# A three-fold fetch of sample operands, issued as three transfers of 32 rows

## The chip, the cores and the metric

The kernel runs on one core of a Trainium2 chip. The metric is the device time of one launch in microseconds (us), the median of several runs. The engines work side by side, each through its own list of instructions in order: TensorE (PE in the profile, its weight loads PEld), VectorE (DVE), ScalarE (ACT), GpSimd (POOL) and SyncE (SP), which here does nothing but issue transfers.

## The reference

One inference step of a two-layer recurrent decoder trunk, on 256 prompt tokens (one sequence) and 64 sample tokens (8 sequences of 8 tokens), width 2048, all in float32. Layer 0 mixes with gated DeltaNet heads (8 of 128 x 128) and GLA heads (4 of 128 x 256); layer 1 is a gated linear recurrence (RG-LRU) with a short convolution. Each layer is a normalisation, one large input projection, the mixer, a gate, and an output projection added to x. The new recurrent states are outputs too. What matters here is the last step of the two mixers for a chunk of sample tokens, the new state:

```python
def _gated_delta_rule(q, k, v, g, beta, S0):
    ...
        S = S * jnp.exp(g_last)[..., None, None] + jnp.einsum('bhck,bhcv->bhkv', k_dec, v_new)

def _gla(q, k, v, gk, S0):
    ...
        S = S * jnp.exp(b_last)[..., None] + jnp.einsum('bhck,bhcv->bhkv', k_dec, v_c)
```

For the sample tokens that is, for each of 8 sequences and each head, the old state scaled by a decay, plus an outer product over 8 tokens.

## The kernel before

All 320 tokens stand as columns, features in partitions. The dense work is 30 groups of 512 output features; a group runs over 8 chunks of 256 input features (`run_group`). A chunk's weights (`wst`, 512 KB) come by one transfer of SyncE (line 209), are split into a rounded part `wh` on ScalarE (line 239) and a remainder `wl` on VectorE (line 240), and are multiplied on TensorE (line 264) with tokens split likewise into `xh` (line 1410) and `xl` (line 1411): three products per tile, `xh wh`, `xl wh` and `xh wl`, which give float32 accuracy. `wst` has three buffers, `wh` and `wl` six each.

Everything else is written as Python generators that hang in queues (`hi`, `lo`, `tails`). Between the matmuls of a group, `slot` advances the queues by one step each, and `wait("name")` lets a number of slots pass that a table gives. So the order of instructions on each engine comes from the order in which the program is traced, with priorities for a few pieces. `behind(i)` ties an instruction to the last matmul traced: it isn't put ahead of that matmul in the order, but it doesn't wait for it by a semaphore. All transfers of SyncE leave from one queue.

The generator `sample_states` computes the new states of the sample tokens. It runs twice in the queue `lo`: `sample_states(0, 16)` for the delta heads, beside the first output projection, and `sample_states(16, 24)` for GLA, beside the last one. Its operands were written earlier to small tensors in device memory, `kt_scratch` (k), `wv_scratch` (v) and `vk_scratch` (v and k together), by SyncE (`to_rows`, line 985): 32 rows of tokens, each of which holds four tokens' vectors one behind the other.

- `fetch` (line 996) loads one such piece into a tile of 96 partitions: the same 32 rows three times, at partitions 0, 32 and 64, by one transfer whose source pattern begins with three repeats of step zero. There are twelve of them: four `uk` and four `uv` (each 96 rows of 2 KB, 192 KB) and four `uvk` (96 rows of 3 KB, 288 KB). Each name has two buffers.
- `parts` casts the tile to the rounded form (`ukh`, `uvh`, `uvkh`; VectorE, line 1003), and GpSimd replaces one 32-row third by the remainder of k and another by that of v (line 1007), so that one product over 96 rows is the sum of the three products of a split multiplication.
- `spread` (line 1012, GpSimd) makes `uvm`, the v of one block of rows, masked so that one matmul gives four sequences.
- The matmul (line 1112 for delta, `sn`; line 1126 for GLA, `gsn`) gives the outer products, and VectorE adds the decayed old state (`ust`, `ugt`; lines 1116 and 1130). The states come in by SyncE (lines 1060 and 1066) and go out by GpSimd's queue (lines 1119 and 1133).

Of the kernel before, what the change touches and what calls it, by code (L numbers as in the profile page):

```python
# [71 lines left out]
def hybrid_step(ctx, tc, x_cols, w_dense, w_small, w_lr, w_gate, par_a, par_b, par_c, gains, head_rows,  # L72
# [3 lines left out]
    pe, act, dve, pool, sp = nc.tensor, nc.scalar, nc.vector, nc.gpsimd, nc.sync  # L76
# [49 lines left out]
    def behind(i):  # L126
        tc.add_manual_dep(i.ins, marks[-1].name, mybir.DependencyInfo(
            mybir.DependencyClass.NoSync, mybir.DependencyReason.DATA), reason="issue_after")
# [858 lines left out]
    def sample_states(first, last):  # L987
# [5 lines left out]
        def fetch(name, src, off, n, w, bufs):  # L993

            t = ws.tile([R, n, w], F32, name=name, tag=name, bufs=bufs)
            behind(sp.dma_start(t.rearrange("p q w -> p (q w)"), bass.AP(  # L996
                tensor=src.tensor, offset=src.offset + off, ap=[[0, 3], [4 * w, 32], [1, n * w]])))
            return t

        def parts(t, name, n, w, k, v):  # L1000
# [17 lines left out]
        def fetch_unit(v):  # L1018
            if v < 4:
                raw[v] = [fetch("uk", kt_d[v], 0, 4, P, 2), None]  # L1020
                yield from wait("sample_states.1")
                raw[v][1] = fetch("uv", wv_d[v], 0, 4, P, 2)
                yield from wait("sample_states.1")

        def fetch_half(i):
            if 2 * i < last:
                v, r = divmod(2 * i, 4)
                raw["g", i] = fetch("uvk", vk_d[v - 4], 3 * P * r, 2, 3 * P, 2)
# [886 lines left out]
    rows = fw.tile([P, NT], F32, name="frows")  # L1915
# [3 lines left out]
    for m, f, n in ((0, 0, 1), (0, 1, 1), (0, 2, 2), (1, 0, 2), (1, 2, 2), (2, 0, 2), (2, 2, 2), (3, 2, 2)):  # L1919
        t = ob[m][:, f:f + n]  # L1920
# [64 lines left out]
```

## Time and profile before

| | |
|---|---|
| runs | 998.79, 994.37, 994.74 us; median 994.74 |
| the profiled execution | 994.33 us, its span 992.6 us |
| TensorE busy | 969.5 us (98% of the span) |
| VectorE, ScalarE, GpSimd busy | 707.5, 532.9, 220.2 us |
| bytes moved | 171.62 MB, a mean of 173 GB/s |
| queue of SyncE (q1) | 59716 packets, 160.35 MB |

The profile shows one execution. Times within it count from the start of the span, and what the run takes beyond the span (1.73 us here) lies around it. A line such as "L996" is line 996 of the kernel. The text after the change reads single rows: an engine's timeline gives start, length, engine, line and operation with output and inputs, then in brackets how long the engine stood idle before it and which instruction or transfer is held to have released it.

### The profile page before, as it was taken

To read this page: it belongs to the slowest core of one execution; us is meant where nothing else is said; L and a number is where in the kernel's file an instruction comes from. 1 tells how busy PE (TensorE), PEld (TensorE's weight loads), DVE (VectorE), ACT (ScalarE), POOL (GpSimd) and SP (SyncE) were. 2 spreads that over 40 slices of the span, in tenths; PEclk is the share of its full clock that TensorE was granted. 3 is DMA by queue.
4 is the path that set the end of the run, shared out by engine and by line. 5 is a ranking of instruction groups with operands and counts; after the bars stand their busy time and mean duration, and the time that the engine had idled before them with its cause. 6 is when DMAs were issued, how large, how long until landed. Compare 5 with 4: busy or idle time off the path is not lost.

```text
span 992.6 us, 18768 instructions
## 1 busy us (share of the span) xinstructions
PE 969.5 (98%) x6917; PEld 950.5 (96%) x6917; DVE 707.5 (71%) x1485; ACT 532.9 (54%) x1083; POOL 220.2 (22%) x365
## 2 busy tenths in 40 slices
PE   9999999999999999999998999999999999999995
PEld 9989999999999999999978999999999999999995
DVE  7898887666545556779667789877969668766753
ACT  8556874457333444776423345447685885333441
POOL 4520018503282111120104234200010000052200
PEclk9999999999999999999999999999999999999998
DMA  8544444534455366445486877654545445568742
GB/s 297 178 134 135 133 130 157 143 131 135 127 157 163 93 218 228 133 111 151 157 258 204 241 258 229 228 165 146 158 124 189 130 127 169 165 216 276 258 155 106
DMA packets 64792, 171.62 MB, mean 173 GB/s; under 512 B 16345, under 2 KB 21997, under 8 KB 64189
## 3 DMA queue, kind: packets, MB, share of 16 engines
q1 hardware_dynamic: 59716, 160.35, 51.8%
q0 software_dynamic: 2720, 8.66, 2.3%
q10 hardware_dynamic: 2264, 1.42, 0.5%
q8 instruction: 54, 0.88, 0.4%
q14 instruction: 38, 0.30, 0.1%
HBM read 155.73 MB, written 14.68 MB: 172 GB/s over the span
## 4 chain that ended last, share of the span: by engine, by line
PE 44%; DVE 2%; DMA 2%; POOL 1%; issue 1%; SPq 0%; DVEq 0%; ACT 0%; POOLq 0%
PE acc L264 42%; DMA uv<-wv_scratch 1%; DMA ugt<-in_state_gla_dram 1%; POOL uvkh L1007 1%; DVE wl L240 1%; DVE ob L1921 0%; PE lg L1549 0%; PE lg L1550 0%; PE lg L1548 0%; PE gsn L1126 0%; PE sn L1112 0%; DVE xh L1410 0%; PE fsp L1670 0%; POOL gso L1166 0%; SPq L996 0%
## 5 line engine op out<-in xcount | busy, mean ns | idle before, releaser
L264 PE MATMUL acc<-xh,wh 128*128 128x320 f32 x1920 | 601.2, 313 | 2.7 <-DVE slab L355 1.2
L264 PE MATMUL acc<-xl,wh 128*128 128x320 f32 x1920 | 595.1, 310 | 1.3 <-DVE xl L1411 1.3
L264 PE MATMUL acc<-xh,wl 128*128 128x320 f32 x1920 | 594.5, 310 | 1.7 <-DVE wl L240 1.5
L239 ACT ACTIVATE wh<-wst 128x512 fp32r<-128x512 f32 x479 | 278.7, 623 | 312.5 <-PE acc L264 252.0
L240 DVE TENSOR_TENSOR wl<-wst,wh 128x512 fp32r<-128x512 f32 x479 | 332.3, 726 | 146.2 <-ACT wh L239 143.8
L264 PEld LDWEIGHTS acc<-xh,wh 128*128 128x128 f32 x1920 | 361.6, 188 | 6.0 <-issue 1.9
L264 PEld LDWEIGHTS acc<-xl,wh 128*128 128x128 f32 x1920 | 361.6, 188 | 3.4 <-DVE xl L1411 1.8
L264 PEld LDWEIGHTS acc<-xh,wl 128*128 128x128 f32 x1920 | 360.8, 188 | 3.5 <-DVE wl L240 2.8
L463 DVE SCALAR_TENSOR_TENSOR yc<-slab,pa,yc 128x344 f32<-128x344 f32 x72 | 42.6, 606 | 1.5 <-ACT yc L101 1.1
L698 POOL TENSOR_TENSOR xi<-xi,tmp 128x60 f32<-128x60 f32 (+24 forms) x62 | 26.2, 423 | 4.8
L1577 POOL MEMSET aa<- 128x32 f32 x4 | 0.7, 164 | 117.7 <-ACT rr L1564 66.7
L696 POOL TENSOR_TENSOR tmp<-ab,xi 128x60 f32<-128x60 f32 (+24 forms) x62 | 24.6, 398 | 4.9
L1007 POOL TENSOR_TENSOR uvkh<-uvk,uvkh 32x256 fp32r<-32x256 f32 (+1 forms) x8 | 12.2, 1526 | 58.3 <-DMA ugt<-in_state_gla_dram 51.0
L1012 POOL TENSOR_TENSOR uvm<-uvh,rm 96x512 fp32r<-96x512 f32 x16 | 20.9, 1327 | 1.6 <-PE sn L1112 1.3
L753 POOL TENSOR_TENSOR so<-so,mhalf 128x4 f32<-128x4 f32 x4 | 4.5, 1121 | 71.9 <-DVE so L752 71.9
L467 ACT ACTIVATE qkv<-yc 128x256 f32<-128x256 f32 x24 | 10.0, 416 | 18.7 <-DVE yc L463 18.6
L1116 DVE SCALAR_TENSOR_TENSOR ust<-ust,es,sn 128x128 f32<-128x128 f32 x64 | 17.7, 338 | 2.9 <-PE sn L1112 1.8
L101 ACT ACTIVATE yc<-slab,pa 128x344 f32<-128x344 f32 x24 | 13.3, 576 | 10.9 <-DVE slab L355 10.7
L1508 DVE SCALAR_TENSOR_TENSOR yc<-slab,pb,yc 128x344 f32<-128x344 f32 x32 | 17.5, 572 | 0.7 <-ACT yc L1506 0.6
L1119 POOL DMA_DIRECT2D out_s_delta_dram<-ust x8 | 6.0, 751 | 53.9 <-DVE ust L1116 53.9
L1130 DVE SCALAR_TENSOR_TENSOR ugt<-ugt,ebs,gsn 128x256 f32<-128x256 f32 x32 | 14.1, 472 | 4.3 <-PE gsn L1126 4.3
L354 DVE TENSOR_TENSOR slab<-acc,rb 128x256 f32<-128x256 f32 x36 | 14.9, 415 | 2.8 <-PE acc L264 2.6
(463 smaller groups left out, 1006.8 us busy)
## 6 DMA issues: line engine op xcount, KB each, us to landing
wst<-in_w_dense_dram SPq DMA_DIRECT2D x237, 512.0 KB
st<-in_state_delta_dram SPq DMA_DIRECT2D x8, 512.0 KB
st<-in_state_gla_dram SPq DMA_DIRECT2D x4, 1024.0 KB
ust<-in_state_delta_dram SPq DMA_DIRECT2D x8, 512.0 KB
out_s_delta_dram<-ust POOLq DMA_DIRECT2D x8, 512.0 KB, 5.1
ugt<-in_state_gla_dram SPq DMA_DIRECT2D x8, 512.0 KB
out_s_gla_dram<-ugt POOLq DMA_DIRECT2D x8, 512.0 KB, 5.0
x0r<-in_x_cols_dram SPq DMA_DIRECT2D x8, 320.0 KB
```

The source lines that it names most:

```text
L239: act.activation(h, wst[i][:, a, :], AF.Copy)
L240: env["last_split"] = dve.tensor_sub(l, wst[i][:, a, :], h.bitcast(F32))
L264: mm = pe.matmul(o, (h, h, l)[j][:, fs], (xh, xl, xh)[j][k], start=(k == 0 and j == 0), stop=(k == KT - 1 and j == 2))
L354: dve.tensor_mul(xp[:, 3:259], xp[:, 3:259] if acc is None else acc[:, :256], rb[:, :256])
L463: dve.scalar_tensor_tensor(y[:, :n], xp[:, j:j + n], pa[:, ft, j:j + 1], y[:, :n], op0=OP.mult, op1=OP.add)
L696: behind(pool.tensor_mul(tv, ab[:, j, j + 1:, None].to_broadcast([P, m, w]), xi[:, j:j + 1, :w].to_broadcast([P, m, w])))
L698: behind(pool.tensor_add(xi[:, j + 1:, :w], xi[:, j + 1:, :w], tv))
L1007: pool.tensor_sub(o, t[rows, :, cols], o.bitcast(F32))
L1012: pool.tensor_mul(m, src.bitcast(F32)[:, None, :].to_broadcast([R, 4, P]), rm4[:R, :, None].to_broadcast([R, 4, P]))
L1116: dve.scalar_tensor_tensor(s_, s_, es[:, col:col + 1], ps[:, b, :], op0=OP.mult, op1=OP.add)
L1130: dve.scalar_tensor_tensor(s_, s_, ebs[:, h, 4 * hb + b + i:4 * hb + b + i + 1], ps[:, i * 256:(i + 1) * 256], op0=OP.mult, op1=OP.add)
L1508: dve.scalar_tensor_tensor(y[:, :n], xp[:, j:j + n], pb[:, ft, 2 + j:3 + j], y[:, :n], op0=OP.mult, op1=OP.add)
```

## The change

In `fetch`, the one transfer into 96 partitions becomes three transfers of the same 32 source rows, each into its own 32 partitions. Each of them is tied behind the last traced matmul, as the one was. `parts` and everything that reads the tile stay as they are.

```diff
         def fetch(name, src, off, n, w, bufs):
 
             t = ws.tile([R, n, w], F32, name=name, tag=name, bufs=bufs)
-            behind(sp.dma_start(t.rearrange("p q w -> p (q w)"), bass.AP(
-                tensor=src.tensor, offset=src.offset + off, ap=[[0, 3], [4 * w, 32], [1, n * w]])))
+            rows = bass.AP(tensor=src.tensor, offset=src.offset + off, ap=[[4 * w, 32], [1, n * w]])
+            for c in range(3):
+                behind(sp.dma_start(t[32 * c:32 * c + 32].rearrange("p q w -> p (q w)"), rows))
             return t
```

## The prediction

> **What bounds the kernel now.** I read the head of the page first, then the chain that ended last, then the windows, and only then single rows at the places where the fetches stand.
>
> ```profile
> span 992.6 us, 18768 instructions
> ...
> PE 969.5 (98%) x6917; PEld 950.5 (96%) x6917; DVE 707.5 (71%) x1485; ACT 532.9 (54%) x1083; POOL 220.2 (22%) x365
> ...
> PE acc L264 42%; DMA uv<-wv_scratch 1%; DMA ugt<-in_state_gla_dram 1%; POOL uvkh L1007 1%; DVE wl L240 1%; DVE ob L1921 0%; PE lg L1549 0%; PE lg L1550 0%; PE lg L1548 0%; PE gsn L1126 0%; PE sn L1112 0%; DVE xh L1410 0%; PE fsp L1670 0%; POOL gso L1166 0%; SPq L996 0%
> ```
>
> TensorE has work in 969.5 of 992.6 us: everything that could be won by feeding it better, in the whole kernel, is 23.1 us. The chain is matmuls (L264) with a few foreign links, and two of these belong to the change: the landing of uv, and the chain around uvkh. The windows say where TensorE idles around the fetches:
>
> ```profile
> 510.00:520.00 10.00, 9.39 (x78) 7.94 (x77) 5.43 (x15) 2.39 (x6) 0.74 (x2) 1.00 0.79 231
> 520.00:530.00 10.00, 7.56 (x47) 6.64 (x45) 8.13 (x11) 1.55 (x3) 7.88 (x6) 1.00 0.62 193
> ...
> 560.00:580.00 20.00, 20.00 (x136) 19.86 (x135) 15.46 (x25) 7.41 (x12) 5.01 (x5) 1.00 0.88 279
> ```
>
> After the window come its length, busy time of PE, PEld, DVE, ACT, POOL, the granted clock, the DMA share and GB/s. TensorE idles 2.44 us (10.00 less 7.56) at 520 to 530, where the first uk and uv are cast; at 560 to 580, among the later ones, it is full. The clock is 1.00 in these slices, so none of it is a throttle.
>
> **Place A, the first uk and uv.** Rows of the SyncE, VectorE and GpSimd timelines (start, length, instruction, in brackets the idle time before it and its releaser), and the waits of TensorE from 515 to 531 (us in total, times, longest):
>
> ```profile
> 510.55 0.80 SPq L996 DMA_DIRECT2D uk<-kt_scratch  x1
> 511.39 0.74 SPq L996 DMA_DIRECT2D uv<-wv_scratch  x1
> ```
> ```profile
> 520.51 0.42 DVE L1003 CAST ukh<-uk 96x512 fp32r<-96x512 f32 x1
> 522.77 0.42 DVE L1003 CAST uvh<-uv 96x512 fp32r<-96x512 f32 x1 [1.84 <-DMA uv<-wv_scratch]
> 523.11 0.32 DVE L1410 CAST xh<-ob 128x320 fp32r<-128x320 f32 x1
> ...
> 524.35 1.39 DVE L1410 CAST xh<-ob 128x320 fp32r<-128x320 f32 x1
> ```
> ```profile
> 521.06 1.29 POOL L1007 TENSOR_TENSOR ukh<-uk,ukh 32x512 fp32r<-32x512 f32 x1 [4.63 <-DVE ukh L1003]
> 523.33 2.23 POOL L1007 TENSOR_TENSOR uvh<-uv,uvh 32x512 fp32r<-32x512 f32 x1 [0.97 <-PE acc L264]
> 525.63 5.17 POOL L1012 TENSOR_TENSOR uvm<-uvh,rm 96x512 fp32r<-96x512 f32 x4
> ```
> ```profile
> PE acc L264 <- DVE xl L1411: 1.3, 2, 0.8
> PE acc L264 <- DVE xh L1410: 1.1, 2, 0.8
> ```
>
> uv (192 KB) is issued at 511.39, and the cast that waits for it starts at 522.77, so it took some 11.3 us to land. VectorE, which works in order, stands at its cast for 1.84 us; behind that cast are the xh and xl of the next group, and TensorE waits 1.3 + 1.1 us for them: the idle 2.4.
>
> **Place B, the first two uvk.** The same views at 860 to 880, with a link of the chain (start, length):
>
> ```profile
> 862.39 0.72 SPq L996 DMA_DIRECT2D uvk<-vk_scratch  x1
> ...
> 865.30 0.72 SPq L996 DMA_DIRECT2D uvk<-vk_scratch  x1
> 866.07 0.44 SPq L1066 DMA_DIRECT2D ugt<-in_state_gla_dram  x1
> ```
> ```profile
> 866.07 6.03 DMA ugt<-in_state_gla_dram
> ```
> ```profile
> 871.37 0.56 DVE L1003 CAST uvkh<-uvk 96x768 fp32r<-96x768 f32 x1 [4.80 <-DMA uvk<-vk_scratch]
> ...
> 878.91 0.72 DVE L1003 CAST uvkh<-uvk 96x768 fp32r<-96x768 f32 x1 [2.74 <-DMA uvk<-vk_scratch]
> ```
> ```profile
> 872.15 5.96 POOL L1007 TENSOR_TENSOR uvkh<-uvk,uvkh 32x256 fp32r<-32x256 f32 x2 [51.02 <-DMA ugt<-in_state_gla_dram]
> ```
> ```profile
> 879.27 0.50 PE L1126 MATMUL gsn<-uvkh,uvm 96*128 96x256 f32 x2 [1.34 <-POOL uvm L1012]
> ```
>
> The first uvk (288 KB, issued 862.39) is there at 871.3, the second (issued 865.30) at 878.9: 9 and 13.5 us. A 512 KB state transfer, ugt, was issued on the same queue at 866.07, after the second uvk, and the chain has it landed at 872.10, 6.8 us before that uvk. TensorE then waits 1.34 us for the tile that GpSimd makes of the first. So the fetches don't wait for the queue as a whole: they are slow by themselves. What is special in them is the source pattern, which begins with three repeats of step zero.
>
> The Trainium skill, "DMA: Bandwidth & Descriptors", section "Rules for kernel authors", says that an outermost dimension of size c under 16, and it names the zero-stride broadcast, confines a transfer to at most c of 16 engines. By that rule each fetch here runs on three, and a piece of 32 rows on sixteen; the overtaking by ugt agrees, though no row here shows single engines. The sum by this rule is the forecast's.
>
> **The change, part by part.**
> 1. Landing. The same bytes move, in pieces whose pattern begins with 32 rows. In the window of A, transfers ran at 231 GB/s: uk and uv (384 KB) are 1.7 us of that, and 1 MB of backlog from two weight loads before them (512 KB each) some 4.5 us. So uv lands at about 511.4 + 1.7 + 4.5 = 517.6 (an estimate), with VectorE there at 520.93: the wait of 1.84 us is gone unless the gain is under 1.84 of 11.29 us. At B the first uvk needs to land 1.34 us sooner for the whole of B's wait to go, out of 9 us.
> 2. What A is worth. VectorE gains up to 1.84 us, and TensorE behind it too. What is late next is GpSimd beside VectorE: the xh cast that takes 0.32 us alone takes 1.39 next to a subtraction of L1007, and that subtraction 2.23 in place of 1.29. With uvh cast at 520.93, the xh cast behind it meets the first subtraction (521.06 to 522.35) that it missed before; if it stands until that ends, it ends at 522.4 in place of 523.43, 1.0 us gained. If VectorE and GpSimd took turns all the way (GpSimd 2 x 1.29; VectorE an estimated 1.9 for five instructions of 0.3 to 0.6 net; from 520.93), the second xh would end at 525.4 in place of 525.74: 0.35 us. Ends 0.35 and 1.84; I take 1.4, between the one collision and none, since the 1.39 row shows one long cast in two, not all.
> 3. What B is worth. TensorE's wait of 1.34 us goes: the cast moves from 871.37 to about 866.6, where VectorE begins to wait, so 4.8 us sooner; even with L1007 at its slow 5.96 us and one uvm of 1.3 (5.17 / 4), the tile is ready near 874.5, and TensorE comes for it at 877.93. Ends 0.5, if the subtractions slow down by another 4 us, and 1.34; I take 1.3. The second cast's 2.74 us on VectorE go too, worth nothing more: TensorE reaches that tile only after the first.
> 4. The other nine fetches. The answer for the fetch's line lists who waited for it, and it is the three casts above:
>
> ```profile
> DVE uvkh L1003: 7.5, 2
> DVE uvh L1003: 1.8, 1
> ```
>
> So landing sooner is worth nothing for the rest.
> 5. SyncE. Two more issues for each of 12 fetches.
>
> ```profile
> L996 SPq EVENT_SEMAPHORE  x5: 17/17/17, 558.1 to 897.1; - x5
> L996 SPq DMA_DIRECT2D uk<-kt_scratch x4: 705/709/795, 510.5 to 588.0; - x4
> ```
> ```profile
> L209 SPq DMA_DIRECT2D wst<-in_w_dense_dram x237: 322/328/1073, 8.3 to 958.4; - x119
> ```
> ```profile
> SPq L209 <- DVE wl L240: 592.4, 198, 7.9
> ```
>
> An issue costs 0.33 us (a weight load, plain rows) to 0.71 (the present fetch). Three pieces cost 1.0 to 2.1 us where one cost 0.71, so what stands behind on SyncE, which is the next weight or state load, goes out 0.3 to 1.4 us later, 24 issues in all. It is covered because SyncE waits 592 us for VectorE to free weight buffers. Where the cover is thin, weights are late for ScalarE:
>
> ```profile
> 572.24 1.15 ACT L239 ACTIVATE wh<-wst 128x512 fp32r<-128x512 f32 x2 [3.67 <-DMA wst<-in_w_dense_dram]
> ```
>
> There ScalarE waits 3.67 us and TensorE still doesn't idle (20.00 of 20.00 at 560 to 580). If the cover were gone, 0.3 to 1.4 us would be paid at each fetch. I cost it at 0, and 1.4 us at one place for the range.
> 6. Waits. The casts now need three completions in place of one: no row prices that on VectorE; the nearest is SyncE's own semaphore instruction of 17 ns beside the fetch. 12 x 2 x 17 ns is 0.4 us, off the path but at A and B: 0.1 us.
> 7. Less traffic on the engines that held the fetches: weights behind a fetch land sooner. TensorE, full there, wins nothing: 0.
>
> Sum: -1.4 - 1.3 + 0.1 = -2.6 us. The profiled execution took 994.33 us (span 992.6 and 1.73 around it); it becomes 991.7. The median shown is 994.74, 0.4 above, and gives 992.1; I put 991.8. About 0.5% (5 us) is what a measurement of this kernel can tell from no change, so this counts as within.
>
> The same section of the Trainium skill's page "DMA: Bandwidth & Descriptors" also speaks against the change: transfers under 64 KB are mostly overhead and many small ones should be one, and halves of the partitions bring nothing, since they run one behind the other on the same engines. By it the sum would be no gain at best; as a mechanism here it is the third rival, priced there from rows.
>
> **The rivals.**
> - The gain is eaten (993.3 to 995.5, say 994.3). A gives only its 0.35 because GpSimd holds VectorE, and B's wait comes back as a slower subtraction beside the weight splits (the two of L1007 at 872.15 took 5.96 us, where one of twice the size took 1.29). For it: the 1.39 row. Against: B has 3.4 us of slack.
> - All idle time around the fetches goes (989.9). The 2.44 and 1.34 us and the 0.61 of 510 to 520 make -4.4. For it: xh and xl are all that TensorE waits for there. Against: 1.84 us is all that VectorE can win at A.
> - Slower: the pieces go one after another, each with a completion of its own. Nearest row:
>
> ```profile
> xd_scratch<-xt POOLq DMA_DIRECT2D x8, 32.0 KB, 3.3
> ```
>
>   Six pieces of 3.3 us are 19.8, so uv lands at 530.4 and VectorE waits 9.4 us in place of 1.84: +7.6 us, 1002. It decides from the point where six pieces take over 12 us together. Against: ugt overtook uvk, so transfers do overlap.
> - The transfer was not slow by its pattern, and the same bytes land as late as before: 994.3 to 995.7, by the SyncE issues. Against: ugt again.
>
> **How the numbers follow.** Forecast (990.3 to 993) 0.58; eaten 0.14; all idle time 0.10; one after another, or another loss of over 5 us through late weights, 0.08; no sooner landing 0.10. Below 989.8 lie half of the second rival, which ends at that bound, and a little more won elsewhere, 0.08 in all; slower by over 5 us 0.08; within 0.84. The range goes from a little past that rival, 989.3, to 996.6, the eaten case plus one unhidden 1.4 us and the spread of 0.4 between profile and median.
>
> **What would show it.** In the changed profile the cast of uvh at A follows that of ukh with no DMA wait; the two uvkh casts have none, or under 1 us; the chain has no uv link of 11 us; gsn's first wait for uvm is gone; 520 to 530 shows PE near 9.0 and 870 to 880 near 10. SyncE shows 36 rows of L996; each at 0.33 us says that the pattern made it 0.71. Wrong would be: uv still past 520.9; xh casts of over 1 us that took A's gain back; weight waits on ScalarE that reach TensorE; or an order of instructions on VectorE that differs from today's.

## The result and the profile after

The changed kernel takes 987.82 us (median of 4 runs, 987.60 to 988.23) against 994.56 (median of 4, 994.32 to 998.79). The ratio is 0.9926, with a 95% interval of 0.9904 to 0.9947: 0.74% faster, 6.7 us, outside the predicted range (989.3 to 996.6). The profiled execution has a span of 985.8 us, 6.8 less than before.

The head of the page after, and its chain:

```profile
span 985.8 us, 18794 instructions
...
PE 966.3 (98%) x6917; PEld 948.2 (96%) x6917; DVE 707.0 (72%) x1485; ACT 532.8 (54%) x1083; POOL 214.8 (22%) x365
...
PE acc L264 43%; DMA ust<-in_state_delta_dram 1%; DVE ob L1922 0%; PE lg L1550 0%; PE lg L1551 0%; PE lg L1549 0%; PE gsn L1127 0%; DVE wl L240 0%; PE gpo L1362 0%; DVE ust L1117 0%; DVE xl L1412 0%; DVE xl L1415 0%; PE sn L1113 0%; PE fsp L1671 0%; POOL gso L1167 0%
```

The link through uv is gone, and TensorE's busy time fell by 3.2 us beside 3.6 us of idle time. Windows of the kernel before, then of the one after (columns as in the prediction):

```profile
530.00:540.00 10.00, 9.81 (x66) 9.49 (x66) 8.61 (x16) 4.51 (x7) 0.81 (x1) 1.00 0.47 151
870.00:880.00 10.00, 8.65 (x60) 8.39 (x59) 5.53 (x10) 2.20 (x4) 7.72 (x4) 1.00 0.70 222
```
```profile
520.00:530.00 10.00, 9.90 (x67) 9.59 (x66) 8.12 (x12) 4.63 (x7) 6.62 (x6) 1.00 0.69 220
530.00:540.00 10.00, 10.00 (x70) 9.96 (x69) 7.73 (x19) 2.63 (x5) 3.43 (x3) 1.00 0.65 206
...
870.00:880.00 10.00, 10.00 (x71) 10.00 (x70) 6.16 (x10) 2.89 (x6) 5.72 (x5) 1.00 0.69 200
```

At A TensorE went from 7.56 and 9.81 to 9.90 and 10.00, at B from 8.65 to 10.00. Read the counts in brackets too: 47 + 66 matmuls before, 67 + 70 after, from 520 to 540. A full window holds 70 to 71, so 24 matmuls are 3.4 us, though the busy times differ by only 2.53. In the trace before, matmuls follow each other every 0.15 us where nothing holds them, but each is recorded as 0.31 us long, and as 0.38 to 0.42 behind a gap at A; so busy time hides some of what is lost.

VectorE's timeline at A after the change:

```profile
519.00 0.32 DVE L1411 CAST xh<-ob 128x320 fp32r<-128x320 f32 x1
...
519.83 0.49 DVE L1412 TENSOR_TENSOR xl<-ob,xh 128x320 fp32r<-128x320 f32 x1
520.23 0.41 DVE L1004 CAST ukh<-uk 96x512 fp32r<-96x512 f32 x1
520.57 0.32 DVE L1411 CAST xh<-ob 128x320 fp32r<-128x320 f32 x1
520.92 1.50 DVE L1412 TENSOR_TENSOR xl<-ob,xh 128x320 fp32r<-128x320 f32 x1
...
523.55 0.41 DVE L1004 CAST uvh<-uv 96x512 fp32r<-96x512 f32 x1
```

Neither cast waits for a transfer. But the order is another one. Before, both casts stood ahead of the last two xh and xl, for which TensorE waits. After, ukh stands behind the first of these two pairs, and uvh behind both. The program text didn't ask for that: VectorE's list, which the build orders, differs in 16 places, all between 520 and 554 or 871 and 891 us, while those of TensorE, ScalarE and GpSimd are unchanged. So the change has two parts, transfers and an order.

To see where time comes from I compare the start of the same matmul of L264 in two traces: how much sooner it comes than in the trace before is the lead. A column is the change of the lead over one stretch (times of the trace before, in us): 90 to 105, long ahead of the first fetch; 520 to 530, over A; 868 to 893, over B. Elsewhere the lead moves by less than 0.8 us, but for the kernel with interleaved rows. In the last row TensorE's list differs between 507 and 521 too, so its A is read from 500 to 541. The last column is the ratio of times with its interval (1 is no change).

| kernel | 90–105 | A | B | median | ratio |
|---|---|---|---|---|---|
| changed | 1.55 | 3.44 | 1.65 | 987.82 | 0.9926 (0.9904–0.9947) |
| changed, again | 1.54 | 3.43 | 1.65 | 987.81 | 0.9926 (0.9908–0.9945) |
| before, again | 1.55 | −1.15 | −0.08 | 994.30 | 0.9996 (0.9983–1.0008) |
| three pieces, old order | 0.01 | −0.03 | 1.65 | 992.92 | 0.9981 (0.9971–0.9991) |
| one transfer, new order | 1.56 | 3.43 | −0.20 | 990.61 | 0.9963 (0.9950–0.9976) |
| three pieces, pattern 2 x 16 | 0.01 | 3.43 | 1.65 | 988.01 | 0.9932 (0.9918–0.9947) |
| one transfer, 96 outermost, old order | 1.54 | −0.03 | 1.64 | 992.45 | 0.9970 (0.9957–0.9983) |
| one transfer, repeat inside, old order | 1.54 | −1.21 | 1.64 | 992.20 | 0.9970 (0.9958–0.9982) |
| three pieces, 2 outermost, rows interleaved, old order | 1.56 | −3.96 | −5.08 | 1007.78 | 1.0125 (1.0102–1.0147) |
| three pieces, old order, GpSimd held back | 0.00 | 2.97 | 1.64 | 989.74 | 0.9940 (0.9925–0.9954) |
| one transfer, 96 outermost, new order | 1.54 | 3.43 | 1.64 | 988.75 | 0.9930 (0.9918–0.9942) |
| scratch written three times, new order | 1.55 | −0.21 | 1.64 | 993.07 | 0.9969 (0.9956–0.9982) |

Each kernel ran beside runs of the kernel before. The median of those was 994.56 to 994.73 us, but 995.78 for the last three rows, so rows are compared by the ratio. Two executions that took far longer, 1585.14 us of the kernel before and 2442.37 of the one transfer with 96 outermost, are left out of the ratios.

### The profile page after: what moved, and what is told of

Same layout as the page of the kernel before. It is cut to its first block, busy times and chain, and to the rows that moved or that the text cites. A ratio compares the mean times of both kernels' runs of the same rounds, so it can differ in the third digit from the quotient of the medians.

```text
span 985.8 us, 18794 instructions
## 1 busy us (share of the span) xinstructions
PE 966.3 (98%) x6917; PEld 948.2 (96%) x6917; DVE 707.0 (72%) x1485; ACT 532.8 (54%) x1083; POOL 214.8 (22%) x365
## 4 chain that ended last, share of the span: by engine, by line
PE 46%; DVE 2%; issue 1%; DMA 1%; POOL 0%; ACT 0%; DVEq 0%; SPq 0%; ACTq 0%; POOLq 0%
PE acc L264 43%; DMA ust<-in_state_delta_dram 1%; DVE ob L1922 0%; PE lg L1550 0%; PE lg L1551 0%; PE lg L1549 0%; PE gsn L1127 0%; DVE wl L240 0%; PE gpo L1362 0%; DVE ust L1117 0%; DVE xl L1412 0%; DVE xl L1415 0%; PE sn L1113 0%; PE fsp L1671 0%; POOL gso L1167 0%
## 5 line engine op out<-in xcount | busy, mean ns | idle before, releaser
L264 PE MATMUL acc<-xh,wh 128*128 128x320 f32 x1920 | 601.0, 313 | 1.3 <-DVE slab L355 1.2
L264 PE MATMUL acc<-xh,wl 128*128 128x320 f32 x1920 | 594.3, 310 | 2.2 <-DVE wl L240 2.2
L264 PE MATMUL acc<-xl,wh 128*128 128x320 f32 x1920 | 594.6, 310 | 0.1
L264 PEld LDWEIGHTS acc<-xh,wh 128*128 128x128 f32 x1920 | 361.0, 188 | 4.3 <-ACT smpQ L470 1.8
L264 PEld LDWEIGHTS acc<-xh,wl 128*128 128x128 f32 x1920 | 360.2, 188 | 4.1 <-DVE wl L240 3.4
L264 PEld LDWEIGHTS acc<-xl,wh 128*128 128x128 f32 x1920 | 360.7, 188 | 2.0 <-issue 0.4
L1008 POOL TENSOR_TENSOR uvkh<-uvk,uvkh 32x256 fp32r<-32x256 f32 (+1 forms) x8 | 9.0, 1124 | 55.9 <-DMA uvk<-vk_scratch 48.1
L101 ACT ACTIVATE yc<-slab,pa 128x344 f32<-128x344 f32 x24 | 13.3, 575 | 11.3 <-DVE slab L355 11.2
```

What stands on the lines that cost most here:

```text
L101: return act.activation(out, in_, AF.Identity, scale=scale)
L264: mm = pe.matmul(o, (h, h, l)[j][:, fs], (xh, xl, xh)[j][k], start=(k == 0 and j == 0), stop=(k == KT - 1 and j == 2))
```

## The experiments

**The kernel before, again.** No edit.

> The kernel before, once more. The traces of before and after differ by 1.5 us at 92 to 95 us, long before the first fetch: the clock granted to TensorE was 0.50 there before and 1.00 after, with the same instructions on TensorE, ScalarE and GpSimd. Theory C1 (a matter of the single execution): some of these executions come out near 993.0 and the profile may show 1.00 at 92. Theory C2 (it goes with the program): every execution stays within 0.3 us of 994.4, and the profile shows 0.50 at 92 to 95 again.

It ran at 994.30 us, as theory C1 has it. Its twelve runs span 992.69 to 997.17, so single executions of this kernel differ by 4.5 us. Two windows each, of the trace before, of this one, and of the changed kernel:

```profile
93.00:94.00 1.00, 1.00 (x5) 1.00 (x5) 1.00 (x3) 0.00 (x0) 0.00 (x0) 0.50 0.32 119
526.00:528.00 2.00, 1.20 (x7) 0.97 (x8) 2.00 (x2) 0.00 (x0) 2.00 (x3) 1.00 0.55 220
```
```profile
93.00:94.00 1.00, 1.00 (x9) 1.00 (x8) 1.00 (x3) 0.00 (x0) 0.00 (x0) 1.00 0.11 45
526.00:528.00 2.00, 2.00 (x9) 2.00 (x9) 2.00 (x2) 0.00 (x0) 2.00 (x3) 0.50 0.20 75
```
```profile
93.00:94.00 1.00, 1.00 (x9) 1.00 (x8) 0.97 (x4) 0.00 (x0) 0.00 (x0) 1.00 0.38 148
526.00:528.00 2.00, 2.00 (x16) 2.00 (x14) 0.61 (x2) 1.72 (x3) 2.00 (x3) 1.00 0.50 189
```

The granted clock stands behind the five engines. At 93 to 94 us it is 0.50 in the first trace and 1.00 in the second, of the same kernel: these are the 1.55 us of the first stretch (the dip), and they belong to the execution, not to the change. At 526 to 528 the second trace has 0.50, just behind A's idle time, and loses 1.15 us more there. The changed kernel, whose TensorE doesn't idle there, has 1.00. The Trainium skill, "TensorE: Matmul & The Clock Gate", section "Part 1: The HAM clock gate", has the clock at half after at least one idle window of about 3.4 us, in windows that run freely. That it comes in one execution and not in another agrees; but TensorE was not idle here, only half busy (0.78 and 1.05 us in the two windows of 2 us from 522 on), and no row shows a window's bounds.

**Three pieces, VectorE's old order at A and B.** The changed kernel, with the order written out:

```diff
+    in_order(("xl", 13), ("wl", 240), ("cast", 0), ("cast", 1), ("xh", 14), ("wl", 241), ("xl", 14), ("xh", 15), ("xl", 15), ...)
+    in_order(("xl", 30), ("cast", 8), ("xh", 31), ("wl", 424), ("wl", 425), ("xl", 31), ("wl", 426), ..., ("cast", 9), ...)
```

> The three transfers as in the changed kernel, but VectorE's list at the first uk and uv and at the first uvk put back in the order of before (the casts ahead of the xh and xl that TensorE waits for). TensorE's list is the same in all. Theory L (sooner landing is the gain): uv has landed when VectorE comes for it, no wait of the cast, and of 3.4 us at the first uk and uv 1.0 to 3.4 stay won, all of 1.6 at uvk: 987.8 to 990.2. Theory O (the order of VectorE's list is the gain at the first uk and uv): the xh and xl wait behind casts and GpSimd's subtractions again, most of 3.4 us comes back, uvk stays won: 990.5 to 991.2. The clock at 92 may add 1.5 to either.

992.92 us, just above what theory O gives with the 1.5 us of the clock (990.5 to 992.7; this trace has the clock at 0.50 at 93 to 94). VectorE and GpSimd at A, and TensorE's waits from 515 to 531:

```profile
520.71 0.41 DVE L1014 CAST uvh<-uv 96x512 fp32r<-96x512 f32 x1
521.04 0.32 DVE L1424 CAST xh<-ob 128x320 fp32r<-128x320 f32 x1
521.28 1.79 DVE L246 TENSOR_TENSOR wl<-wst,wh 128x512 fp32r<-128x512 f32 x1
522.99 1.58 DVE L1425 TENSOR_TENSOR xl<-ob,xh 128x320 fp32r<-128x320 f32 x1
524.50 1.16 DVE L1424 CAST xh<-ob 128x320 fp32r<-128x320 f32 x1
```
```profile
520.92 1.60 POOL L1020 TENSOR_TENSOR ukh<-uk,ukh 32x512 fp32r<-32x512 f32 x1 [4.63 <-DVE ukh L1014]
522.60 1.63 POOL L1020 TENSOR_TENSOR uvh<-uv,uvh 32x512 fp32r<-32x512 f32 x1
524.30 4.94 POOL L1025 TENSOR_TENSOR uvm<-uvh,rm 96x512 fp32r<-96x512 f32 x4
```
```profile
PE acc L271 <- DVE xl L1425: 2.1, 2, 1.3
...
PE acc L271 <- DVE xh L1424: 0.6, 1, 0.6
```

The cast of uvh waits for nothing, so the pieces did land sooner; yet TensorE still waits 2.7 us here for xl and xh, and A gains −0.03. VectorE starts its wl 2 us sooner, but now beside GpSimd, and wl, xl and xh take 1.79, 1.58 and 1.16 us. The two engines take turns: wl ends at 523.07, after the first subtraction (522.52), xl at 524.57, after the second (524.23), and xh at 525.66, after the first of the four products (about 525.5, a quarter of 4.94 us from 524.30). In the kernel before this xh ended at 525.74. That the 1.84 us of the wait are used up to within 0.03 us is a chance of these lengths. B gains its full 1.65 in the old order. Its landing, by the issue of the first uvk and the cast that waits for it:

```profile
862.27 1.31 SPq L1008 DMA_DIRECT2D uvk<-vk_scratch  x3
```
```profile
867.53 0.56 DVE L1014 CAST uvkh<-uvk 96x768 fp32r<-96x768 f32 x1 [0.75 <-DMA uvk<-vk_scratch]
```

That is 5.3 us from the first issue to the cast, against 9.0 before.

**One transfer, the new order.** The kernel before, with the list order of the changed one at A and B:

```diff
+    in_order(("xl", 13), ("wl", 240), ("xh", 14), ("wl", 241), ("xl", 14), ("cast", 0), ("xh", 15), ("xl", 15), ("wl", 242), ("wl", 243), ("cast", 1), ("wl", 244))
+    in_order(("xl", 30), ("xh", 31), ("xl", 31), ("wl", 424), ("wl", 425), ("cast", 8), ("wl", 426), ("wl", 427), ("cast", 9), ("wl", 428))
```

> The one transfer of before, but VectorE's list at the first uk and uv and at the first uvk in the order of the changed kernel. Theory O: the first uk and uv gain the whole 3.4 us although uv lands as late as before, because nothing that TensorE needs stands behind the cast; at uvk the cast still waits about 4 us and gsn for uvm, so nothing is won there: 991.1, or 989.6 if the clock at 92 is 1.00. Theory L: without sooner landing at most 1 us is won: 993.5 to 994.5.

990.61 us: A gains 3.43 without any change to the transfers. B gains nothing, since the fetches still land late:

```profile
865.98 0.56 DVE L1010 CAST uvkh<-uvk 96x768 fp32r<-96x768 f32 x1 [2.93 <-DMA uvk<-vk_scratch]
...
872.82 0.56 DVE L1010 CAST uvkh<-uvk 96x768 fp32r<-96x768 f32 x1 [5.08 <-DMA uvk<-vk_scratch]
```
```profile
880.00:890.00 10.00, 8.38 (x58) 8.14 (x57) 8.14 (x17) 5.53 (x10) 0.62 (x1) 1.00 0.84 292
```

The wait for uvm has gone, and the lead grows by 1.6 us there; but TensorE now idles 1.62 us at 880 to 890, where it waits for a wh, and the lead is lost again. VectorE's 5.08 us at the second cast are the likely cause. A later run has the same order with a fetch that lands soon, and does not idle there.

**A pattern of 2 x 16 rows.** The changed kernel with another way to write the same addresses:

```diff
-            rows = bass.AP(..., ap=[[4 * w, 32], [1, n * w]])
+            rows = bass.AP(..., ap=[[64 * w, 2], [4 * w, 16], [1, n * w]])
```

> Three transfers as in the changed kernel, with the same list of instructions on every engine, but the 32 source rows written as 2 x 16 rows, so that the source pattern begins with a dimension of two where before it began with three. Theory D (a short outermost dimension makes the landing late): uv lands 11 us or more after its issue, the uvk casts wait at least the 4.8 and 2.7 us of before; with the new order little is lost at the first uk and uv (0 to 1 us), 1.3 us or more at uvk: 989.2 to 992. Theory N (one transfer in three pieces lands sooner, whatever the pattern): 987.8, no waits of the casts. The Trainium skill, DMA: Bandwidth & Descriptors, Rules for kernel authors, would put each piece on two engines, slower than the three of before.

988.01 us, A and B as in the changed kernel. Read alone, this speaks against the reading that a short outermost dimension is what makes a fetch slow. But 64 w is sixteen steps of 4 w, so both patterns name the same rows in the same order, and may reach the hardware as one. The trace speaks for that. SyncE issues the first three uvk in 1.31 us, as in the changed kernel. And by the packet records, where only a uvk fetch has packets of 3 KB, up to 17 packets of the first uvk are under way at once, so it doesn't run two wide. This run didn't test theory D. Hence the next three.

**Which pattern is slow.** All three in VectorE's old order, where the casts wait and so show the landing. In all three, the sample states come from other rows, or rows in another order.

```diff
 one transfer, 96 outermost:
-    ap=[[0, 3], [4 * w, 32], [1, n * w]]
+    ap=[[w, 96], [1, n * w]]
 one transfer, repeat inside:
-    ap=[[0, 3], [4 * w, 32], [1, n * w]]
+    ap=[[4 * w, 32], [0, 3], [1, n * w]]
 three pieces, 2 outermost, rows interleaved:
-    ap=[[4 * w, 32], [1, n * w]]
+    ap=[[4 * w, 2], [8 * w, 16], [1, n * w]]
```

> One transfer of 96 rows as before, whose source pattern begins with 96 rows (step of one row of w) and has no repeats; every instruction list is that of the kernel before. It reads other rows of the scratch, so the sample states are of other data. Theory D (the fetch was slow because its pattern began with three): uvh's cast has no DMA wait, the first uvkh cast under 1.5 us of wait (lands within 5.5 us of its issue, against 9.0), gsn's wait of 1.34 gone; A still idles 2.3 to 2.7 us by the old order of VectorE's list, so about 992.9 like the three pieces in the old order. Theory S (a single transfer of 192 to 288 KB is slow by itself, pieces are what helped): waits of 1.8, 4.8 and 2.7 as before, 994.3 to 994.7.

> One transfer of 96 rows whose source pattern begins with 32 rows and repeats each three times behind that, so the order of rows in the tile is another (sample states of other data); instruction lists are those of the kernel before. Theory D: lands as fast as the kernel with 96 rows outermost, no uvh wait, first uvkh wait under 1.5 us, about 992.9. Theory Z (reading the same rows three times is what is slow, wherever the repeat stands): waits of 1.8, 4.8 and 2.7 as before, 994.3 to 994.7. Theory S: as before too.

> Three pieces in the old order of VectorE's list, whose pattern begins with two, then 16 rows at every second row, which cannot be folded into one dimension of 32 as that of the kernel before it could (rows come in another order, so the sample states are of other data). Theory D, by the outermost dimension: each piece stands on two engines, so 288 KB on two where the old fetch had three: 1.5 times 9.0 us, the first uvk lands some 13 us after its issue, its cast waits about 9 us, and the time is 996 or more. Theory N (any three pieces are fast): first uvkh waits 0.5 to 1 us, uvh none, 992.9 like the three pieces in the old order.

The issue of the first uvk and the start of its cast, which waits for it, in this order of kernels (for the interleaved pieces, the cast of uvh too):

```profile
860.18 0.33 SPq L996 DMA_DIRECT2D uvk<-vk_scratch  x1
```
```profile
865.12 0.56 DVE L1003 CAST uvkh<-uvk 96x768 fp32r<-96x768 f32 x1 [0.73 <-DMA uvk<-vk_scratch]
```
```profile
862.52 0.56 SPq L996 DMA_DIRECT2D uvk<-vk_scratch  x1
```
```profile
867.98 0.56 DVE L1003 CAST uvkh<-uvk 96x768 fp32r<-96x768 f32 x1 [1.27 <-DMA uvk<-vk_scratch]
```
```profile
868.88 1.92 SPq L1008 DMA_DIRECT2D uvk<-vk_scratch  x3
```
```profile
523.07 0.42 DVE L1014 CAST uvh<-uv 96x512 fp32r<-96x512 f32 x1 [3.88 <-DMA uv<-wv_scratch]
...
879.31 0.56 DVE L1014 CAST uvkh<-uvk 96x768 fp32r<-96x768 f32 x1 [5.92 <-DMA uvk<-vk_scratch]
```

From issue to cast: 4.9 us with 96 rows outermost, 5.5 with 32 outermost and the repeat inside, 10.4 with 2 outermost, against 9.0 before. The 10.4 begin with 1.92 us for three issues, where one took 0.72; from the end of the issues it is 8.5 us against 8.3, which doesn't tell two from three. The packet records do. For the 96 packets of the first uvk:

| outermost dimension | packets under way at once, mean | at most | first packet to end of last, us |
|---|---|---|---|
| 3 (before) | 2.6 | 5 | 6.0 |
| 2, interleaved, three pieces | 2.0 | 3 | 7.3 |
| 96 | 7.1 | 17 | 2.2 |
| 32, repeat inside | 5.3 | 16 | 2.7 |
| 32, three pieces, old order | 12.0 | 18 | 2.1 |

So neither the size of a single transfer nor reading rows three times makes a fetch slow: it is the short outermost dimension. This is the Trainium skill's rule ("DMA: Bandwidth & Descriptors", "Rules for kernel authors"), and these runs agree: most of the time three and two packets are under way where the pattern begins with 3 and 2. Two in place of three would make the packets' time half as long again, 9.0 us; 7.3 were measured. The time, 1007.78 us, came out above the 996 expected: A loses 3.96, 4.6 us go between A and B, where the old fetches cost nothing, and B loses 5.08. The kernels with fast single transfers run at 992.45 and 992.20, as the pieces in the old order do.

**The changed kernel again.**

> The changed kernel once more, beside runs of the kernel before on the same chip. If 1.5 us of the 6.8 us between the two profiled spans is the half clock at 92 to 95 us, which comes in some executions whatever the kernel, this profile shows either the dip and a span near 987.4, or no dip and 985.8; the ratio of the times stays at 0.9915 to 0.994. If the change itself removed the dip, no execution of it shows 0.50 there.

987.81 us, span 986.2, no dip at 92 to 95. The kernel of the 2 x 16 pattern, whose instruction lists are the same, does show the dip (clock 0.50 at 93 to 94) and has a span of 987.4. So the dip comes and goes with and without the change.

**Old order, GpSimd held back.** The three pieces in the old order; the first two subtractions of `parts` wait for the group's last xl:

```diff
+    for n in (0, 1):
+        tc.add_manual_dep(kept["low", n], kept["xl", 15].name, ...)
```

> The three pieces in the old order of VectorE's list, with the first two subtractions of the split on GpSimd (ukh, uvh) held back until the last xl of the group is made. In the kernel without this, VectorE at A ran its wl in 1.79, xl in 1.58 and xh in 1.16 us beside GpSimd, and TensorE waited 2.1 + 0.6 us. Theory G (the two casts cost little, it is GpSimd beside VectorE that costs): with GpSimd quiet these take 0.7, 0.5 and 0.3, TensorE's waits for xh and xl fall to 1.0 or less, the step at A is 2.4 to 3.4 and the time 989.5 to 990.5. Theory O (the two casts that stand ahead of xh and xl cost the time by themselves): waits of 2.0 to 2.7 stay, 992.9.

989.74 us. VectorE at A, and the first subtraction on GpSimd:

```profile
521.54 0.41 DVE L1014 CAST uvh<-uv 96x512 fp32r<-96x512 f32 x1
...
522.12 0.68 DVE L246 TENSOR_TENSOR wl<-wst,wh 128x512 fp32r<-128x512 f32 x1
522.72 0.48 DVE L1426 TENSOR_TENSOR xl<-ob,xh 128x320 fp32r<-128x320 f32 x1
523.12 0.32 DVE L1425 CAST xh<-ob 128x320 fp32r<-128x320 f32 x1
```
```profile
524.10 1.29 POOL L1020 TENSOR_TENSOR ukh<-uk,ukh 32x512 fp32r<-32x512 f32 x1 [6.96 <-DVE xl L1426]
```

The same wl, xl and xh in the same order take 0.68, 0.48 and 0.32 us in place of 1.79, 1.58 and 1.16, and A gains 2.97 of the 3.43. So with the operands there in time, what A costs in the old order is nearly all GpSimd beside VectorE; the place of the casts matters because the cast is what lets GpSimd start. The Trainium skill, "GPSIMD Engine Reference", section "Specifications", says that GpSimd shares its way to SBUF with VectorE, and contends with instructions that run in a 2-port mode or have two SBUF inputs. wl and xl have two, and agree; xh has one and takes 1.16 us in place of 0.32 all the same, and no row shows its mode.

**One transfer with 96 outermost, the new order.** The two edits above together, `[[w, 96], [1, n * w]]` (other rows of the scratch) and the new order.

> The single transfer of 96 rows with 96 outermost (other rows of the scratch, so the sample states are of other data), with VectorE's new order at A and B. If the two effects add, A gives the 3.4 of the order and B the 1.65 of the landing, and the time is that of the changed kernel, 987.5 to 988.5, with 24 issues fewer on SyncE. If the three pieces matter beyond landing and order, it stays near the one transfer in the new order, 990.6.

988.75 us, a little above the 987.5 to 988.5 expected; the ratio is 0.9930 against 0.9926. A gains 3.43 and B 1.64, with 24 issues fewer, and TensorE is full where the same order with late fetches idled 1.62 us:

```profile
880.00:890.00 10.00, 10.00 (x72) 10.00 (x71) 8.55 (x16) 5.83 (x10) 0.54 (x1) 1.00 0.72 256
```

So it was the late landing that cost those. The parts add: at A and B fast landing and order are the whole of the change, and the pieces as such bring nothing beside them.

**The scratch written three times, fetched by one plain transfer, new order.** A version without pieces and with the reference's data:

```diff
-        sp.dma_start(bass.AP(..., offset=d.offset, ap=[[w, 4], [4 * w, 32], [1, w]]), t)
+        for c in range(3):
+            sp.dma_start(bass.AP(..., offset=d.offset + 128 * w * c, ap=[[w, 4], [4 * w, 32], [1, w]]), t)
...
-    ap=[[0, 3], [4 * w, 32], [1, n * w]]
+    ap=[[4 * w, 96], [1, n * w]]
```

> Each scratch of sample operands written three times, and fetched by one transfer of 96 plain rows, with VectorE's new order. Twenty more writes of the scratch on SyncE and three matmuls at another place in TensorE's list. If that is hidden, 987.5 to 988.5 as the changed kernel; if the extra writes delay weights, 989 to 992.

993.07 us, above both forecasts, where the kernel before took 995.78; by the ratio, 0.9969, it wins less than half of what the changed kernel wins. B is won, but the first uk goes out at 513.49, behind the extra writes, and its cast waits again, now ahead of an xh, so that nothing is won over A:

```profile
523.88 0.42 DVE L1011 CAST ukh<-uk 96x512 fp32r<-96x512 f32 x1 [0.77 <-DMA uk<-kt_scratch]
524.23 0.32 DVE L1421 CAST xh<-ob 128x320 fp32r<-128x320 f32 x1
```

## Why the prediction was wrong

**Step 2, the worth of A, failed.** It put 1.4 us on an end to the wait for uv, between 0.35 and 1.84, with VectorE's list as it stood. Both halves are wrong. In that list, sooner landing is worth nothing at A: −0.03 in two kernels where the wait of 1.84 was gone, below my lower end of 0.35. I had the collision of VectorE with GpSimd in hand (the xh of 1.39 us), but took 0.4 us off for it. In fact the engines take turns all the way, the picture that I gave only 0.35 us: wl, xl and xh meet both subtractions and the first product, which I had left out, and grow from 1.48 us together to 4.53. It is the wl that the first subtraction holds, not the xh that I named, which takes its 0.32 us. And the list did not stand: the build moved the casts behind the xh and xl, and that alone gives 3.43. I named another order only as a sign of error, without a price or a chance.

**The size of A** was also misread. I took the idle time, 10.00 less 7.56, for all that could be lost there. The count of matmuls says 3.4 us. Nor are the 23.1 us of the whole kernel a bound, for the same reason. The rival in which all idle time around the fetches goes had the right picture (520 to 530 is at 9.90), but its 4.4 us, A with the 0.61 of 510 to 520 and B, fell short of the measured 5.09 for A and B alone, though the 0.61 is still there.

**Step 1, landing, was right**, and its reason is now shown by the patterns and the packets, no longer only inferred from the overtaking. With 96 rows outermost, uv was issued at 510.00 and its cast ran at 518.58 with no wait: at most 8.6 us, where 11.3 were taken before. **Step 3, B: right in kind**, 1.65 in place of 1.3, and over my upper end of 1.34, which was a wait alone. My lower end was wrong by its own terms: a tile 4 us later than 874.5 is there at 878.5, and leaves 0.8, not 0.5. B doesn't need the new order.

**Step 4, the other fetches: right.** From behind A to ahead of B the lead of the changed kernel goes from 4.95 to 4.92 us.

**Step 5, SyncE: right at 0**, with another price for an issue:

```profile
L998 SPq DMA_DIRECT2D uk<-kt_scratch x12: 410/452/1822, 509.0 to 583.6; - x12
L998 SPq DMA_DIRECT2D uv<-wv_scratch x12: 302/419/430, 511.8 to 585.0; - x12
L998 SPq DMA_DIRECT2D uvk<-vk_scratch x12: 382/421/649, 857.1 to 891.5; - x12
```

36 issues, with a median of 0.42 to 0.45 us where I expected 0.33. Three uv or uvk cost about 1.3 in place of 0.71 (the first three uk 2.75, one of them 1.82), and TensorE loses nothing by it between the places. The first uvk as one transfer of 96 plain rows takes 0.33 and the second 0.42, so it was indeed the pattern that made an issue cost 0.71.

**Step 6** (0.1 us for more waits) is too small for these runs. **Step 7, weights: right.** ScalarE's wait for weights fell from 30.2 to 10.8 us in total, and TensorE gained nothing from it between A and B.

**What no step had** is the clock: 1.55 us of the 6.8 between the two spans belong to a dip that comes in some executions of any of these kernels. Without it the change is worth 5.1 us by the traces. The medians say 6.7. A dip behind A's idle time, seen in two of the five traces of kernels that idle at A in the old order with a fast or an unchanged fetch (clock 0.50 and 0.57, 1.15 and 1.21 us), would be part of the rest. The mean granted clock was recorded for each run, and bears that out: of 79 runs of the kernel before beside these experiments only six are above 0.995, at 993.16 us in the mean; of the ten of the changed kernel in the table's first two rows nine are, at 987.79. Between these the change is worth 5.4 us, near the 5.1 of the traces. So the medians differ by more because the kernel before mostly runs at a lower mean clock; that A's idle time is what lowers it is likely, but not shown for unprofiled runs.

## What to carry to other kernels

A change in the number of transfers can change the order of an engine that it doesn't touch: compare the lists of all engines before the time is put down to the transfer, and give a change of order its own place among the rivals. An early operand can be worth nothing if what it starts on one engine slows down the instructions that the bound engine waits for; ask what the cast releases, not only what it waits for. Read the count of instructions in a window beside the busy time, and profile the same kernel twice before a difference far from the change is explained.

## What the runs showed of the hardware

- The outermost dimension of the source pattern sets how fast a fetch of 288 KB lands. From issue to cast: 4.9 us (96), 5.5 (32, with repeats inside), 5.3 (three pieces with 32), 9.0 (3), 10.4 (three pieces with 2). With 3 and 2 outermost, three and two packets are under way most of the time, with 96 up to 17.
- Beside GpSimd's subtractions and products VectorE took turns with it: its split took 1.79 us in place of 0.68, its subtraction of xl 1.58 in place of 0.48, and its cast of xh 1.16 in place of 0.32.
- TensorE's clock went to 0.50 from 526 to 528 us behind a stretch of half idle time in one execution of a kernel, and stayed at 1.00 in another.
